# Low parts of every second weight tile by an adding DMA from SBUF to SBUF instead of by VectorE

## The chip, the cores and the metric

The kernel runs on one core of one Trainium2 chip. The metric is the device time of one execution in microseconds; the kernel before has a median of 1213.01 us over three runs. One further execution was profiled, and its trace is what is read below.

## What is computed

Four layers of a transformer trunk on 256 tokens of width 1024, all in float32. Each layer has a token mixer (banded attention in layers 0 and 3, gated linear attention in layer 1, differential attention in layer 2), a layer norm, a SwiGLU feed-forward network of hidden width 2816, and another norm. Cut to what matters:

```python
for i in range(DEPTH):                      # 4
    y = mixer(h)                            # x @ w_qkv (or w_in), attention, @ w_o
    h = layer_norm(DN_ALPHA * h + y, ln1_g[i], ln1_b[i])
    g, u = split(h @ ffn_w_gate_up[i])      # [1024, 2 * 2816]
    h = layer_norm(DN_ALPHA * h + (silu(g) * u) @ ffn_w_down[i], ln2_g[i], ln2_b[i])
```

Most of the time is products of 256 tokens with weights that are each read once, 392 tiles of 256 x 512 elements (512 KB).

## The kernel before

**Split products.** TensorE multiplies in float32r, a rounded form of float32. To keep the accuracy, every operand is split into a high part (the value rounded to float32r) and a low part (what the rounding lost). A product is the sum of three: high by low, high by high, low by high. `w_tiles` (L101) makes the parts of a weight tile, which is two k-tiles of 128 rows by 512 columns, so 128 partitions x 1024 elements in SBUF. Its steps: a DMA from SP's queue into `raw` (L109), ScalarE's copy, which rounds it into `wh` (L110), and VectorE's subtraction of the two into `wl` (L111). There are RAWB = 6 buffers for `raw` and WB = 8 each for `wh` and `wl`. The first two tiles (`fine`) are handled one k-tile at a time.

**Row form** (`run_rows`, L141). Tokens stand on the partitions of the result, 512 columns fill a bank. For each token half and k-tile three products are issued: L175 with the low part, L176 and L177 with the high part. Half 1 runs LAG = 10 k-tiles behind half 0, so that each weight tile stays in its buffer for some six tiles' time. This form serves the value projections, the first two chunks of the gate-and-up weights, the output projections (`out_proj`, in an order of its own), and the down projection `w_down`, whose two chunks of 22 k-tiles are 22 tiles per layer, 88 in all. Gated linear attention uses it too, partly with a lag of 4.

**Column form** (`run_cols`, L182). 128 columns of the weights stand on the partitions of the result and all 256 tokens are in the free dimension. The four tiles of a 512-column chunk are made first; then each of four blocks runs over all 8 k-tiles (L196 with the high part, L197 with the low). So a buffer comes free in the last block of its chunk, and eight buffers hold two chunks. Nine chunks of each feed-forward network (36 in all), four of each attention and one of the gated layer run in this form.

**Order of the work.** Work that follows from a finished product is put off by counted half-steps (`defer`, `tick`). The order on each engine is fixed when the kernel is built, by a list scheduler that goes by priorities in program order and by a model of times. On the chip each engine then works through its queue in order and waits on semaphores. A buffer that is taken over makes its writer wait until the last reader of the old contents is done.

**GpSimd's queue** carries little: the layer norms' `rstd_of` (L245, L249, each on a few columns), masks (L408), and the loads of `late_load` (L122 and L123: norm weights, attention biases), which are its only DMAs. Its DMAs are the software queue q0 in the profile; the weight loads from SP are q1.

Of the kernel before, what the change touches and what calls it, by code (L numbers as in the profile page):

```python
# [12 lines left out]
ALU = mybir.AluOpType  # L13
# [12 lines left out]
RAWB = 6  # weight loads under way, 2 k-tiles each  # L26
WB = 8  # split weights on chip, 2 k-tiles each
LAG = 10  # k-tiles that token half 1 runs behind half 0
# Half-steps of the tensor engine (see run_rows) by which work is put off.
# [6 lines left out]
def trunk_kernel(  # L36
# [27 lines left out]
    nc = tc.nc  # L64
# [35 lines left out]
    # ---------------------------------------------------------------- weights  # L100
    def w_tiles(chunk, s, fine=False):  # L101
        """Loads the k-tiles 2s, 2s+1 of a 512-column chunk of the weights and
        returns, per k-tile, their float32r parts (high, low)."""
        raw = wp.tile([P, 2, 512], F32, tag="raw", bufs=RAWB, name=nm("raw"))
        wh = wp.tile([P, 2, 512], F32R, tag="wh", bufs=WB, name=nm("wh"))
        wl = wp.tile([P, 2, 512], F32R, tag="wl", bufs=WB, name=nm("wl"))
        src = chunk[s].rearrange("p (k n) -> p k n", k=2)
        for k in (slice(0, 1), slice(1, 2)) if fine else (slice(0, 2),):
            nc.sync.dma_start(raw[:, k, :], src[:, k, :])  # L109
            nc.scalar.copy(out=wh[:, k, :], in_=raw[:, k, :])  # L110
            nc.vector.tensor_tensor(  # L111
                out=wl[:, k, :],
                in0=raw[:, k, :],
                in1=wh[:, k, :].bitcast(F32),
                op=ALU.subtract,
            )
        return [(wh[:, k, :], wl[:, k, :]) for k in range(2)]

    def late_load(dst, src, seen):
        """A load that is needed late, held back until `seen` is written, to  # L120
        leave the DMA queues to the weights."""
        nc.gpsimd.tensor_copy(dst[:, 0:1], seen)  # L122
        nc.gpsimd.dma_start(dst, src)  # L123

    # Work of the mixers that follows from a finished product is put off by a
    # number of half-steps (one k-tile of 512 columns for one token half), so
    # that the tensor engine has products to run while its inputs are made.
# [13 lines left out]
    def run_rows(chunks, lag=LAG, order=None, fine=0):  # L141
        """Products in row form (tokens on partitions, 512 columns a bank).
        chunks: (weights, k-tiles, src, done); src(kt) gives the high | low
        k-tile of all tokens, done(t, bank) reads the finished product.
        order lists (token half, chunk, k-tile); without it token half 1 runs
        lag k-tiles behind half 0."""
# [35 lines left out]
    def run_cols(w, src, done):  # L182
        """Products in column form: 128 columns of the weights on partitions,
        all 256 tokens in the free dimension. The bank of a column block holds
        the product with the tokens' high parts | with their low parts (high
        weights only), to be added up."""
        wt = []
        for s in range(NKT // 2):
            wt += w_tiles(w, s)
        for blk in (0, 2, 1, 3):  # L190
            b = bank("mm")
            cs = slice(blk * P, (blk + 1) * P)
            for kt in range(NKT):
                wh, wl = wt[kt]
                xk = src(kt)
                nc.tensor.matmul(b, wh[:, cs], xk, start=kt == 0, stop=False)  # L196
                nc.tensor.matmul(  # L197
                    b[:, :256], wl[:, cs], xk[:, :256], start=False, stop=kt == NKT - 1
                )
                if kt == NKT - 1:  # L200
                    done(blk, b)
                if kt % 2:
                    tick(1)
# [3 lines left out]
    # ------------------------------------------------------------- transposes  # L207
    def put(dst, ks, cs, val):
        """Writes val as the high and low parts of k-tiles ks, tokens cs."""
        h = dst[:, ks, cs]  # L210
        nc.scalar.copy(out=h, in_=val)  # L211
        nc.vector.tensor_tensor(  # L212
            out=dst[:, ks, slice(256 + cs.start, 256 + cs.stop)],
            in0=val,
            in1=h.bitcast(F32),
            op=ALU.subtract,
        )

    def split_T(src_cols, dst, t, k0, n):
        """Transposes n [128,128] blocks (row form in src_cols) into the k-tiles  # L220
        k0.. of token half t of dst."""
# [12 lines left out]
    def operand():  # L234
        """High | low parts of 8 k-tiles of all tokens."""
        return slab([P, NKT, 4 * P], F32R)
# [4 lines left out]
    # ------------------------------------------------------------- layer norm  # L241
# [12 lines left out]
    class Norm:  # L254
# [12 lines left out]
        def load(self, seen):  # L267
            """The next of the loads that the norm waits for."""
            if self.loads:
                late_load(*self.loads.pop(0), seen)  # L270
# [61 lines left out]
    def out_proj(OT, w, norm):  # L332
        """The k-tiles that need the last of the mixer's output come late, and
        enough of half 1 after half 0 to cover the norm of half 0."""
# [10 lines left out]
    # ------------------------------------------------- banded softmax attention  # L345
    def attention(xT, wqkv, bias_ap, w_o, norm, diff, src=None, **first):
        """One column block of 128 holds two 64-wide score maps: two heads, or
        the two maps of one differential head."""
# [133 lines left out]
        def turn2(c, pr):  # L482
            """Key block 0: half 0 of both heads, half 1 of both; key block 1:
            half 1 of both heads."""
# [17 lines left out]
        def values2(c, ph, pl):  # L502
            """Values of both heads against the weights of each: the rows of
            the other head are not read."""
# [101 lines left out]
    # ------------------------------------------------- gated linear attention  # L606
    def gla(xT, norm):
# [21 lines left out]
        # Low-rank gate: the columns 0..15 of the stationary tile are the high  # L629
        # parts of w_g1 and 32..47 the low parts (what follows them, the next  # L630
        # k-tile's, gives rows that nothing reads); w_g2 stands in the same
        # rows, so that the second product adds both up, and its bias in row 64.
# [209 lines left out]
    # ----------------------------------------------------------------- swiglu  # L842
# [52 lines left out]
    # ------------------------------------------------------------------ trunk  # L895
# [36 lines left out]
def _layouts(inputs):  # L932
    """Weights laid out chunk by chunk as the kernel reads them, x also with
    its tokens last, and the relative-position tables laid out per (query
    partition p, key column c): the key sits c - 128 - p places after the query."""
# [4 lines left out]
    def tiles(w, pairs=0):  # L940
        """[L, K, N] to [L, chunk, K / 256, 128, 2 * 512]; the first `pairs`
        chunks hold 256 columns of each of the first two parts of that width."""
# [68 lines left out]
```

## Time and profile before

| | |
|---|---|
| median of 3 runs (lowest to highest) | 1213.01 us (1209.94 to 1214.02) |
| span of the profiled execution, first to last instruction | 1209.5 us |
| TensorE busy | 1191.5 us, 99% |
| VectorE busy | 829.6 us, 69% |
| ScalarE busy | 665.5 us, 55% |
| GpSimd busy | 97.7 us, 8% |
| DMA queue q1 (weights), share of 16 engines | 52.1% for 207.64 MB |
| DMA queue q0 (GpSimd's), share | 3.5% for 15.14 MB |
| mean granted TensorE clock, share of full | 0.998 |

Where the profile gives a time of one instruction, it is in ns in the groups and in us in the timelines. A busy TensorE is not TensorE at its peak, as products are pipelined and their ends are modelled; the pace is read from the starts. An idle time in brackets belongs to the engine just before the instruction, with what ended it. The profile gives no time of the profiled execution but its span; the runs' median is 3.5 us above it.

### The profile page before, as it was taken

To read this page: it belongs to the slowest core of one execution; us is meant where nothing else is said; L and a number is where in the kernel's file an instruction comes from. 1 tells how busy PE (TensorE), PEld (TensorE's weight loads), DVE (VectorE), ACT (ScalarE), POOL (GpSimd) and SP (SyncE) were. 2 spreads that over 40 slices of the span, in tenths; PEclk is the share of its full clock that TensorE was granted. 3 is DMA by queue.
4 is the path that set the end of the run, shared out by engine and by line. 5 is a ranking of instruction groups with operands and counts; after the bars stand their busy time and mean duration, and the time that the engine had idled before them with its cause. 6 is when DMAs were issued, how large, how long until landed. Compare 5 with 4: busy or idle time off the path is not lost.

```text
span 1209.5 us, 17080 instructions
## 1 busy us (share of the span) xinstructions
PE 1191.5 (99%) x6224; PEld 993.6 (82%) x6224; DVE 829.6 (69%) x1418; ACT 665.5 (55%) x1169; POOL 97.7 (8%) x188
## 2 busy tenths in 40 slices
PE   7999999999999999999999999999999999999997
PEld 5888888888887888888887778888888888888885
DVE  6687866745656777764667787676466888666644
ACT  6566555643664455663446656556344774665531
POOL 0130000000101000000012110000001200000000
PEclk9999999999999999999999999999999999999999
DMA  9654646556464456555564355665557544655641
GB/s 340 225 189 140 210 173 226 175 176 194 155 229 136 137 195 230 193 184 187 189 226 152 122 168 188 225 198 171 188 185 235 188 126 156 205 208 197 205 143 35
DMA packets 62772, 223.88 MB, mean 185 GB/s; under 512 B 7264, under 2 KB 7776, under 8 KB 62688
## 3 DMA queue, kind: packets, MB, share of 16 engines
q1 hardware_dynamic: 58176, 207.64, 52.1%
q0 software_dynamic: 4512, 15.14, 3.5%
q8 instruction: 49, 0.80, 0.3%
q14 instruction: 35, 0.29, 0.1%
HBM read 221.71 MB, written 1.05 MB: 184 GB/s over the span
## 4 chain that ended last, share of the span: by engine, by line
PE 94%; DVE 2%; ACT 2%; DMA 1%; POOL 0%; issue 0%; SPq 0%; POOLq 0%; DVEq 0%; ACTq 0%
PE mm L196 28%; PE mm L175 15%; PE mm L176 15%; PE mm L197 15%; PE mm L177 15%; PE tp L422 2%; PE tp L224 2%; ACT k L445 1%; PE tp L491 1%; DVE k L430 1%; DMA raw<-in_a_qkv_dram 1%; DVE wl L111 0%; PE tp L512 0%; PE tp L514 0%; PE tp L513 0%
## 5 line engine op out<-in xcount | busy, mean ns | idle before, releaser
L111 DVE TENSOR_TENSOR wl<-raw,wh 128x1024 fp32r<-128x1024 f32 (+1 forms) x394 | 476.0, 1214 | 180.6 <-ACT wh L110 177.7
L196 PE MATMUL mm<-slab,wh 128*128 128x512 f32 x1568 | 555.6, 397 | 0.0
L110 ACT CAST wh<-raw 128x1024 fp32r<-128x1024 f32 (+1 forms) x394 | 406.4, 1047 | 196.7 <-PE mm L177 185.2
L197 PE MATMUL mm<-slab,wl 128*128 128x256 f32 x1568 | 440.8, 281 | 0.0
L196 PEld LDWEIGHTS mm<-slab,wh 128*128 128x128 f32 x1568 | 294.3, 188 | 71.1 <-issue 4.6
L175 PE MATMUL mm<-wl,slab 128*128 128x512 f32 x784 | 311.5, 397 | 7.9 <-DVE wl L111 7.9
L177 PE MATMUL mm<-wh,slab 128*128 128x512 f32 x784 | 307.4, 392 | 0.0
L176 PE MATMUL mm<-wh,slab 128*128 128x512 f32 x784 | 307.2, 392 | 0.0
L197 PEld LDWEIGHTS mm<-slab,wl 128*128 128x128 f32 x1568 | 296.5, 189 | 0.7 <-issue 0.3
L175 PEld LDWEIGHTS mm<-wl,slab 128*128 128x128 f32 x784 | 147.8, 189 | 41.1 <-DVE wl L111 8.5
L177 PEld LDWEIGHTS mm<-wh,slab 128*128 128x128 f32 x784 | 147.6, 188 | 31.7 <-DVE slab L212 0.8
L176 PEld LDWEIGHTS mm<-wh,slab 128*128 128x128 f32 x784 | 147.8, 189 | 30.4 <-issue 1.8
L869 DVE TENSOR_TENSOR k<-mm,k 128x256 f32<-128x256 f32 x144 | 60.6, 421 | 82.9 <-ACT k L868 82.9
L868 ACT COPY k<-mm 128x256 f32<-128x256 f32 x144 | 53.7, 373 | 71.4 <-PE mm L197 71.1
L871 ACT ACTIVATE k<-k 128x256 f32<-128x256 f32 x72 | 29.8, 414 | 46.7 <-DVE k L869 46.7
L245 POOL TENSOR_SCALAR sm<-mv 128x1 f32<-128x1 f32 x16 | 14.1, 883 | 500.4 <-DVE mv L300 500.4
L211 ACT CAST slab<-k 128x256 fp32r<-128x256 f32 (+1 forms) x76 | 31.8, 418 | 40.9 <-DVE k L875 37.4
L212 DVE TENSOR_TENSOR slab<-k,slab 128x256 fp32r<-128x256 f32 (+1 forms) x76 | 33.0, 435 | 23.1 <-ACT slab L211 23.1
L445 ACT ACTIVATE k<-k,nmx 128x128 f32<-128x128 f32 x96 | 42.5, 444 | 8.4 <-DVE nmx L441 8.3
L211 ACT CAST slab<-tp 128x512 fp32r<-128x512 f32 (+1 forms) x56 | 27.1, 495 | 26.6 <-PE tp L224 24.5
L430 DVE CUSTOM_DVE_ANT_0 k<-tp,k 128x128 f32<-128x128 f32 x96 | 28.6, 353 | 10.1 <-PE tp L422 9.0
L212 DVE TENSOR_TENSOR slab<-tp,slab 128x512 fp32r<-128x512 f32 (+1 forms) x56 | 30.6, 569 | 4.6 <-ACT slab L211 4.5
(133 smaller groups left out, 669.5 us busy)
## 6 DMA issues: line engine op xcount, KB each, us to landing
raw<-in_w_gu_dram SPq DMA_DIRECT2D x176, 512.0 KB, 4.4
raw<-in_w_down_dram SPq DMA_DIRECT2D x88, 512.0 KB, 4.2
raw<-in_a_qkv_dram SPq DMA_DIRECT2D x46, 512.0 KB, 4.7
raw<-in_b_in_dram SPq DMA_DIRECT2D x24, 512.0 KB, 3.6
raw<-in_c_qkv_dram SPq DMA_DIRECT2D x24, 512.0 KB, 3.6
raw<-in_a_o_dram SPq DMA_DIRECT2D x16, 512.0 KB, 3.9
k<-in_a_bias_dram POOLq DMA_DIRECT2D x16, 256.0 KB, 4.5
lng<-in_ln_g_dram POOLq DMA_DIRECT2D x8, 512.0 KB, 5.7
```

The source lines that it names most:

```text
L110: nc.scalar.copy(out=wh[:, k, :], in_=raw[:, k, :])
L111: nc.vector.tensor_tensor(out=wl[:, k, :], in0=raw[:, k, :], in1=wh[:, k, :].bitcast(F32), op=ALU.subtract,)
L175: nc.tensor.matmul(b, xh, wl, start=first, stop=False)
L176: nc.tensor.matmul(b, xh, wh, start=False, stop=False)
L177: nc.tensor.matmul(b, xl, wh, start=False, stop=last)
L196: nc.tensor.matmul(b, wh[:, cs], xk, start=kt == 0, stop=False)
L197: nc.tensor.matmul(b[:, :256], wl[:, cs], xk[:, :256], start=False, stop=kt == NKT - 1)
L211: nc.scalar.copy(out=h, in_=val)
L212: nc.vector.tensor_tensor(out=dst[:, ks, slice(256 + cs.start, 256 + cs.stop)], in0=val, in1=h.bitcast(F32), op=ALU.subtract,)
L445: nc.scalar.activation(pr[:, m, SL[t]], pr[:, m, SL[t]], AF.Exp, bias=nmx[:, t, m : m + 1], accum_out=sm[:, t, m : m + 1],)
L868: nc.scalar.copy(out=lo, in_=b[:, 256:])
L869: nc.vector.tensor_tensor(out=lo, in0=b[:, :256], in1=lo, op=ALU.add)
```

## The change

`w_tiles` numbers its tiles. For tiles with an even number above 8 that are not `fine`, VectorE's subtraction is left out. ScalarE writes the negated raw tile, rounded to float32r, into `wl` (which is the negated high part), and a DMA issued on GpSimd's queue adds `raw` onto it, from SBUF to SBUF, so that `wl` holds raw minus high again. The other tiles are as before. Comments and docstrings were also blanked out, and the added lines move all lines behind them by a few; that part of the diff is left out here.

```diff
+    units = [0]
+
     def w_tiles(chunk, s, fine=False):
...
         src = chunk[s].rearrange("p (k n) -> p k n", k=2)
+        units[0] += 1
+        by_dma = not fine and units[0] > 8 and units[0] % 2 == 0
         for k in (slice(0, 1), slice(1, 2)) if fine else (slice(0, 2),):
             nc.sync.dma_start(raw[:, k, :], src[:, k, :])
             nc.scalar.copy(out=wh[:, k, :], in_=raw[:, k, :])
+            if by_dma:
+                nc.scalar.mul(wl[:, k, :], raw[:, k, :], -1.0)
+                nc.gpsimd.dma_start(wl[:, k, :], raw[:, k, :], accum_op=ALU.add)
+                continue
             nc.vector.tensor_tensor(
                 out=wl[:, k, :],
                 in0=raw[:, k, :],
```

## Rows read from the trace of the kernel before

**Rows 1.** The page's first part: busy us, share of the span, instructions.

```profile
PE 1191.5 (99%) x6224; PEld 993.6 (82%) x6224; DVE 829.6 (69%) x1418; ACT 665.5 (55%) x1169; POOL 97.7 (8%) x188
```

**Rows 2.** TensorE's waits: engine line <- releaser: us in total, times, longest us.

```profile
PE mm L175 <- DVE wl L111: 7.9, 2, 6.5
...
PEld tp L578 <- DVE k L565: 2.8, 7, 0.9
...
PEld tp L422 <- DVE slab L396: 2.6, 10, 0.4
...
PEld tp L224 <- DVE h L319: 1.1, 4, 0.3
```

**Rows 3.** The page's costliest groups: busy us, mean ns | idle before, releaser.

```profile
L111 DVE TENSOR_TENSOR wl<-raw,wh 128x1024 fp32r<-128x1024 f32 (+1 forms) x394 | 476.0, 1214 | 180.6 <-ACT wh L110 177.7
...
L110 ACT CAST wh<-raw 128x1024 fp32r<-128x1024 f32 (+1 forms) x394 | 406.4, 1047 | 196.7 <-PE mm L177 185.2
```

**Rows 4.** Timeline of ScalarE in layer 1's down projection: start us, us, what, idle before.

```profile
562.51 1.05 ACT L110 CAST wh<-raw 128x1024 fp32r<-128x1024 f32 x1 [1.67 <-PE mm L177]
565.23 1.05 ACT L110 CAST wh<-raw 128x1024 fp32r<-128x1024 f32 x1 [1.67 <-PE mm L177]
```

**Rows 5.** Timeline of all engines there: two steps of half 0 and half 1.

```profile
567.71 0.39 PE L175 MATMUL mm<-wl,slab 128*128 128x512 f32 x1
...
568.39 0.39 PE L175 MATMUL mm<-wl,slab 128*128 128x512 f32 x1
```

**Rows 6.** Timeline of ScalarE over one chunk of layer 1's gate-and-up columns.

```profile
484.36 1.05 ACT L110 CAST wh<-raw 128x1024 fp32r<-128x1024 f32 x1
...
486.88 2.00 ACT L110 CAST wh<-raw 128x1024 fp32r<-128x1024 f32 x2
...
497.71 0.37 ACT L868 COPY k<-mm 128x256 f32<-128x256 f32 x1
```

**Rows 7.** Stretches: columns, down projection, attention, flat-out loads; columns as headed.

```profile
core 0: us, PE busy (x) PEld busy (x) DVE busy (x) ACT busy (x) POOL busy (x), PEclk, DMA share, GB/s
456.00:522.00 66.00, 66.00 (x383) 58.17 (x382) 45.96 (x73) 41.06 (x72) 2.48 (x4) 1.00 0.61 205
552.00:592.00 40.00, 40.00 (x179) 33.11 (x178) 20.95 (x19) 15.44 (x15) 0.00 (x0) 1.00 0.58 183
40.00:106.00 66.00, 65.93 (x399) 53.96 (x398) 54.68 (x170) 45.87 (x123) 13.85 (x35) 1.00 0.56 184
...
15.00:40.00 25.00, 25.00 (x122) 20.84 (x122) 18.88 (x19) 15.13 (x18) 3.11 (x10) 1.00 0.90 346
```

**Rows 8.** DMA: queue's packets, MB, share; issues, KB, us to landing; the last of 552:592.

```profile
q1 hardware_dynamic: 58176, 207.64, 52.1%
...
lng<-in_ln_g_dram POOLq DMA_DIRECT2D x8, 512.0 KB, 5.7
...
h<-in_x_dram POOLq DMA_DIRECT2D x2, 512.0 KB, 4.2
k<-in_c_bias_dram POOLq DMA_DIRECT2D x8, 128.0 KB, 3.6
...
raw<-in_w_down_dram SPq DMA_DIRECT2D x8, 512.0 KB, 3.5
```

**Rows 9.** GpSimd: its costliest groups, its waits, and a norm's start in its timeline.

```profile
L123 POOL DMA_DIRECT2D k<-in_a_bias_dram x16 | 8.9, 555 | 2.0 <-POOL k L122 2.0
...
POOL k L408 <- DMA k<-in_a_bias_dram: 54.4, 16, 5.9
...
596.37 1.11 POOL L245 TENSOR_SCALAR sm<-mv 128x1 f32<-128x1 f32 x1 [57.42 <-DVE mv L300]
```

## The prediction, made before the changed kernel was run

> **What bounds the kernel now.** I read first how busy each engine is [rows 1]: TensorE is busy for 1191.5 of a span of 1209.5 us, so only 18 us of it are idle, and those include the start and the end. VectorE has 829.6 us of work and ScalarE 665.5 us, neither near the span. The second view is what TensorE and its weight loads wait for [rows 2]: the products of L175 wait for the low parts `wl` twice, 7.9 us in all, of which 6.5 us is one wait at the very start (tile 2 of the first stage, which the change leaves with VectorE, since only tiles after the eighth are touched). The other waits on VectorE are 2.8, 2.6 and 1.1 us in total. So VectorE's subtractions (394 of them, 476.0 us [rows 3]) are hidden almost entirely: taking half of them away frees an engine that nobody waits for. What can still matter is whether the new way to a low part is longer than the cover that the old way has. So the third view is the timeline of the stage with the least cover.
>
> That stage is the down projection. `run_rows` runs token half 1 ten k-tiles (five weight tiles) behind half 0, and there are eight split buffers. So tile i takes over the buffer of tile i-8, which half 1 leaves two tiles before half 0 needs tile i. In the timeline, ScalarE's copy of one tile starts at 562.51 right after it waited 1.67 us for a product of L177 to free the buffer, and the next at 565.23, so one tile lasts 2.72 us [rows 4]. The tile copied at 562.51 is first used by the L175 product at 567.71; the k-tiles that lie between are four of half 0 and four of half 1, 24 products, at 0.68 us for three [rows 5], which is 5.44 us counted from the end of the freeing product. From the start of the copy to the use there are 567.71 - 562.51 = 5.2 us. Before, 1.05 us of copy and 1.22 us of subtraction [rows 3] fill 2.3 us of that, and 2.9 us are spare. This cover, 5.2 us, is the number that decides.
>
> In the column stages the cover is longer. One chunk is four tiles and its buffers come free during the last block of the chunk before. The copy of a chunk's first tile starts at 484.36, its last pair of copies at 486.88 (so the fourth at 487.8), and the chunk is first used at about 497.4, just ahead of L868's copy of the previous chunk's last block at 497.71 [rows 6]. That is 13.0 us for the first tile. The fourth tile is used six k-tiles into its first block, about 2.1 us later (a block of eight is a quarter of a chunk, 2.76 us), so it has 11.7 us.
>
> **The change, part by part.**
>
> *VectorE.* Of 392 tiles those with an even number above 8 go to the new way: 192. VectorE loses 192 x 1.224 = 235 us, worth nothing by itself by [rows 2], at most the 6.5 us of the three waits above that are not at the start.
>
> *ScalarE.* It gains 192 multiplications of 128x1024. Its copy of the same shape takes 1.05 us [rows 3]; I take the same, 202 us, 867 in all. The work that hides them: the column stage at 456 to 522 us has 41.1 us of ScalarE in 66, which becomes 41.1 + 12 x 1.05 = 53.7; the attention stage 45.9 in 66, and eight multiplications make it 54.3 [rows 7]. Both stay below 83%, so I cost it at nothing. Were that cover gone it would be up to 1.05 us per tile on the path.
>
> *The path of a new low part.* Copy 1.05, multiplication 1.05, about 0.1 for two signals, then the adding DMA from issue on GpSimd's queue to landing. No row shows an adding DMA. The nearest: a plain 512 KB load from GpSimd's queue lands in 4.2 us (`h`), one of 128 KB in 3.6 us and a broadcast of 512 KB in 5.7 us; weight loads in the down projection land in 3.5 us [rows 8]. An addition must read its target as well as its source, so I add one more pass of 512 KB through the 16 DMA engines. A pass costs, by q1's row [rows 8], 52.1% of 1209.5 us for 207.64 MB, or 1.59 us for 512 KB, and in the stretch where the loads run flat out, share 0.90 at 346 GB/s [rows 7], 346/0.90 = 384 GB/s, or 1.37 us. So from below 4.2 (the second read hidden), from above 5.7 + 1.6 = 7.3, and below 3.5 would be without any precedent here. I take 4.2 + 1.37 = 5.6 us, nearest to the row of `h`, the same size on the same queue. The path is then 2.2 + 5.6 = 7.8 us, with ends of 6.4 and 9.5.
>
> The Trainium skill (DMA: Bandwidth & Descriptors, Anatomy of one DMA) gives a fit for GpSimd's DMAs of 2.0 us plus the bytes at 436 GB/s, which is 3.2 us for 512 KB. Row and rule differ: the plain one of that size took 4.2 us here. By the rule the path would be 5.4 us and the down projection would lose next to nothing; that is the second rival below.
>
> *Down projection.* The path of 7.8 us against a cover of 5.2 us leaves 2.6 us. A stall of one new tile also lengthens the cover of the next new one, two tiles on, because the buffer that this one needs is freed just ahead of the place of the first stall. So stalls come at every second new tile, not at each. Of 22 tiles per layer the last 14 have the short cover, seven of them new: four stalls of 2.6 us, four layers: 16 x 2.6 = 42 us (ends: 16 x 1.2 = 19 and 16 x 4.3 = 69). Loads of raw tiles have room: a raw buffer is now held until the DMA has landed, some 2.6 us past the old time, but it is refilled six tiles (16 us) ahead and a load takes 3.5 us.
>
> *DMA engines.* A chunk of a column stage has four loads and two additions: 4 x 1.37 + 2 x 2.74 = 11.0 us of all 16 engines, in the 11.05 us that the chunk takes, if a read of the target costs a full pass. With the loads at 1.59 it is 12.7; with an addition at one pass it is 8.2. If the engines can be kept 95% busy (between the 0.90 of the flat-out stretch and full), 11.0 becomes 11.5, so 0.5 us per chunk. The feed-forward layers have 36 such chunks: 18 us (ends 0 and 36 x 1.7 = 61). Attention's chunks last half as long again and are left out; in the down projection the stalls already leave the engines this time.
>
> *GpSimd's queue.* Each addition is one more issue, 0.55 us by L123's row [rows 9], and waits in order for its multiplication. Behind it stand the layer norm's two steps (L245, L249) and the late loads. The norm's chain has no spare: its L245 started at 596.37, at once [rows 9], and TensorE's transposes already wait 0.3 us for L319 four times [rows 2]. A norm that meets a waiting issue is late by up to 2 x 1.05 us; there are 16, the bounds are 0 and 34 us, and I take a quarter, 8 us, since only some will meet one. In attention an issue can also stand behind L408's wait of up to 5.9 us for a bias [rows 9]; the cover there is over 13 us as in the column stage, so nothing.
>
> *Sum:* 42 + 18 + 8 = 68 us on a span of 1209.5, or 1277.5. The median of the three runs is 1213.0, 3.5 us above that span, so 1281 us.
>
> **The rivals.**
>
> *The DMA engines become the bound.* If an addition costs three passes (both reads and the write), a chunk needs 4 x 1.37 + 2 x 4.1 = 13.7 us, at 95% 14.4 instead of 11.05. That is 3.4 us times 36, or 122 us; two tiles of the row stages need 6.8/0.95 = 7.2 instead of 5.44, 1.75 us for each of some 44 pairs of the down projections, 77 us; 200 in all, about 1413 us. For it: the share is already 0.58 to 0.61 in these stages and 3.18 us of two passes per 5.5 us is alone 0.58 more [rows 7]. Against it: I see no row in which the writing side of a load costs time of its own. The Trainium skill (Collectives: The Full Stack, Why ReduceScatter is half of AllGather) says that an addition in a DMA is slower because it needs two source reads and not because of the arithmetic. By that rule it is two passes and the sum above stands; no row here can show it.
>
> *Not slower: the landing fits the cover.* The place is the down projection, and the point is an issue-to-landing time of 3.0 us: below it the path is 5.2 us and no tile is late. Then only VectorE's relief is left, the waits of 6.5 us less what the norms lose, so 1207 to 1213 us. For it: no loads but its own run in that stage, and source and target are both on chip. Against it: not even the 128 KB transfer of that queue landed in under 3.6 us, and the target has to be read first.
>
> *The change does not do what it says.* If the scheduler delays the GpSimd issues or VectorE still carries the work, VectorE's row of L111 would still count 394 and the time would be that of before, 1213 us.
>
> **How the numbers follow.** Forecast, stalls of the down projection with small additions (1235 to 1325): 0.58. DMA engines the bound (1325 to 1450): 0.30. Landing fits: 0.10, of which 0.04 end faster and 0.06 within 0.3%. Not as said: 0.02, no change. A measurement of this kernel can tell about 0.3% from no change. So faster 0.04, same 0.08, slower 0.88. The range from 1225 to 1420 leaves out the 0.12 of no change and below and some 0.07 at the top; it takes in the low end of the landing time (19 us alone, 1232) and the price of the first rival.
>
> **What would show it.** In the profile of the changed kernel, L111 with 202 instructions, 192 of ScalarE's multiplications at 1.05 us and 192 more issues on GpSimd, with 5.6 us to landing. In the down projection, TensorE waiting in L175 for a DMA into `wl`, 2 to 3 us, at every second new tile, with the granted clock at its upper level. In the column stages a DMA share near 0.95 and few waits. The forecast is wrong if the landing takes 3 us or less, or 8 us and more; if TensorE's waits lie in L196 and L197; or if the transposes of L224 carry most of the loss.

## The result, and the profile after

The changed kernel takes 1354.67 us (median of three runs, 1348.56 to 1360.02) against 1213.01: the ratio is 1.117 with a 95% interval from 1.112 to 1.122, or 142 us more. The prediction was 1281 us, in a range from 1225 to 1420. So the direction was right and the size was not: 142 us were lost where 68 were forecast.

The profiled run lasted 1360.0 us with a span of 1358.3. First the page of the changed kernel: busy time (us, share, instructions), the DMA queues (packets, MB, share of the 16 engines), the costliest groups (busy us, mean ns | idle before, releaser) and the issues of the new DMA (KB, us to landing). The low-part products of L175 and L197 are L183 and L205 here, the copy of L110 is L114, the subtraction of L111 is L119; L116 is the new multiplication and L117 the adding DMA.

```profile
PE 1239.8 (91%) x6224; PEld 1015.9 (75%) x6224; DVE 624.1 (46%) x1226; ACT 832.5 (61%) x1361; POOL 250.1 (18%) x380
...
q1 hardware_dynamic: 58176, 207.64, 44.2%
q0 software_dynamic: 32160, 115.82, 43.5%
...
L119 DVE TENSOR_TENSOR wl<-raw,wh 128x1024 fp32r<-128x1024 f32 (+1 forms) x202 | 244.5, 1212 | 312.7 <-ACT wh L114 312.4
...
L117 POOL DMA_DIRECT2D wl<-raw x192 | 166.2, 867 | 872.5 <-ACT wl L116 692.1
...
L116 ACT ACTIVATE wl<-raw 128x1024 fp32r<-128x1024 f32 x192 | 203.8, 1062 | 52.3 <-PE mm L183 47.5
...
wl<-raw POOLq DMA_DIRECT2D x192, 512.0 KB, 7.2
```

The change did what it says: 192 low parts moved, VectorE went from 829.6 to 624.1 us [rows 1], ScalarE gained 192 x 1.062 us. TensorE has the same 6224 products as before, but the span is 148.8 us longer: 100.5 us of that is more idle time (118.5 against 18.0), and 48.3 us is the same products taking longer (1239.8 against 1191.5). These are two losses, and the forecast had only the first.

The next view is what TensorE waits for in the changed kernel (us in total, times, longest us), beside the few waits of before [rows 2].

```profile
PE mm L183 <- DMA wl<-raw: 55.1, 28, 5.1
PE mm L205 <- DMA wl<-raw: 39.2, 23, 4.1
PE mm L183 <- DVE wl L119: 7.3, 2, 6.9
...
PE tp L232 <- DVE h L327: 0.6, 2, 0.3
```

94.3 us of the idle time are 51 waits for the adding DMA, in two places: the row products (L183) and the column products (L205). The wait of 6.9 us at the start is the old one. The norm's transposes (L232) wait 0.6 us, less than before.

By stage, from the first product of a stage's first tile to that of the next, the feed-forward columns of the four layers went from 102.0, 100.1, 102.0, 100.1 to 117.9, 112.2, 115.0, 114.0 us (+55), the down projections from 60.9, 60.9, 60.9, 68.5 to 78.1, 83.8, 75.1, 81.9 (+68), and the rest gained some 26. For layer 1, the columns and then the down projection, first in the kernel before and then in the changed one (headed as in [rows 7]: length, busy time of TensorE, its loads, VectorE, ScalarE and GpSimd, granted clock, DMA share, GB/s):

```profile
441.70:541.80 100.10, 100.10 (x579) 88.22 (x578) 68.20 (x106) 60.52 (x107) 3.56 (x6) 1.00 0.60 204
541.80:602.70 60.90, 60.90 (x274) 50.30 (x273) 35.87 (x44) 27.68 (x30) 2.06 (x2) 1.00 0.58 183
```

```profile
489.70:601.90 112.20, 105.00 (x580) 90.56 (x579) 50.86 (x89) 74.87 (x125) 18.78 (x23) 0.97 0.96 262
601.90:685.60 83.70, 69.56 (x274) 54.95 (x273) 23.95 (x33) 37.55 (x42) 11.10 (x14) 0.90 0.81 213
```

In the kernel before, TensorE was busy for the whole of both stretches, at a clock of 1.00. Now the down projection has 83.70 - 69.56 = 14.1 us of idle time, and its products take 69.56 - 60.90 = 8.7 us longer, at a clock of 0.90 (a tenth of 83.7 is 8.4 us). The DMA share is 0.81 there and 0.96 in the columns.

TensorE's waits for the addition in the four down projections, layer by layer:

```profile
PE mm L183 <- DMA wl<-raw: 10.9, 6, 3.2
...
PE mm L183 <- DMA wl<-raw: 14.1, 6, 5.1
...
PE mm L183 <- DMA wl<-raw: 10.9, 6, 3.1
...
PE mm L183 <- DMA wl<-raw: 7.5, 4, 3.4
```

So the +68 us of the down projections are 43.4 us of waits and 24 us of slower products (TensorE is busy for 266.8 us in these four stretches, 242.7 before). In the feed-forward columns the waits in L205 are 10.7, 7.2, 9.5 and 8.7 us, 36.1 in all, and the slower products are 19 us (423.0 against 404.1).

**The down projection, wait by wait.** TensorE's timeline in layer 0's down projection, from 280 to 327 us (start, us, instruction, idle before): all waits for the addition, and two products between them.

```profile
280.20 0.50 PE L183 MATMUL mm<-wl,slab 128*128 128x512 f32 x1 [3.20 <-DMA wl<-raw]
...
281.95 0.63 PE L183 MATMUL mm<-wl,slab 128*128 128x512 f32 x1
...
285.35 0.39 PE L183 MATMUL mm<-wl,slab 128*128 128x512 f32 x1
...
293.44 0.50 PE L183 MATMUL mm<-wl,slab 128*128 128x512 f32 x1 [0.43 <-DMA wl<-raw]
...
302.44 0.76 PE L183 MATMUL mm<-wl,slab 128*128 128x512 f32 x1 [3.24 <-DMA wl<-raw]
...
315.58 0.50 PE L183 MATMUL mm<-wl,slab 128*128 128x512 f32 x1 [0.66 <-DMA wl<-raw]
...
324.47 0.50 PE L183 MATMUL mm<-wl,slab 128*128 128x512 f32 x1 [3.14 <-DMA wl<-raw]
```

A new tile is due every eight products of L183, 5.44 us. The waits are at two of three: 3.2 us, none, 0.5 us, and again. GpSimd's issues of the additions behind them, from the same timeline:

```profile
288.51 0.85 POOL L117 DMA_DIRECT2D wl<-raw  x1 [12.60 <-ACT wl L116]
293.94 0.85 POOL L117 DMA_DIRECT2D wl<-raw  x1 [4.59 <-ACT wl L116]
300.13 0.85 POOL L117 DMA_DIRECT2D wl<-raw  x1 [5.34 <-ACT wl L116]
```

They land 4.9, 8.4 and 4.8 us after the issue, and the next three likewise (5.1, 8.6, 4.8). The issue at 288.51 lands just ahead of the product of 293.44, the one at 293.94 ahead of that of 302.44. The landing of 8.4 us is the wait of 3.24 us.

The longer landing is the one that meets weight loads. SP's queue of loads stands still while an addition holds the raw buffer that the next load needs (between 285 and 330 us it waits six times for a landing, 30.7 us in all). The addition issued at 288.51 landed at 293.4, and SP at once issued two loads, at 293.45 and 293.87, just ahead of the addition of 293.94:

```profile
293.45 0.80 SPq L113 DMA_DIRECT2D raw<-in_w_down_dram  x2
```

The DMA queues (packets, MB, share of the 16 engines) from 294.5 to 298.0 us, and from 298.5 to 301.0:

```profile
q1 hardware_dynamic: 215, 0.81, 88.3%
...
q0 software_dynamic: 118, 0.47, 94.4%
q1 hardware_dynamic: 34, 0.08, 8.5%
```

In the first stretch GpSimd's queue q0 has no packet (it isn't in the view): the addition moves only when the two loads are nearly through. While the additions that landed in 4.8 to 5.1 us were under way, the engines served loads for 0.4 to 1.5 us, at most the time of one. Over all 192 additions the time to landing goes with the engine time of the loads served meanwhile (a correlation of 0.84, from the packets of the trace). Why the loads go first is not shown.

**The path.** ScalarE in the same stage, for the new tile of 293.44:

```profile
287.15 1.06 ACT L116 ACTIVATE wl<-raw 128x1024 fp32r<-128x1024 f32 x1 [1.31 <-PE mm L183]
288.12 1.03 ACT L114 CAST wh<-raw 128x1024 fp32r<-128x1024 f32 x1
```

The multiplication stands before the copy of the same tile. It waits for the last reader of the old low part (L183); the last reader of the old high part, for which the copy has to wait, is L185 of the same step, two products later. So the copy isn't on the path. From the start of the multiplication the addition is issued 1.36 us later and lands after another 4.9 us, against a cover of 293.44 - 0.43 - 287.15 = 5.9 us: 0.4 us late. With a landing of 8.4 us, and a cover that the short wait has lengthened to 6.6 us, it is the wait of 3.24 us.

**The clock.** The product at 281.95, after the wait of 3.20 us, takes 0.63 us and the one at 285.35 takes 0.39. Two stretches of the same length there, headed as above:

```profile
281.40:284.80 3.40, 3.40 (x9) 2.63 (x9) 0.00 (x0) 0.01 (x1) 0.00 (x0) 0.50 0.99 252
285.00:288.40 3.40, 3.40 (x17) 2.77 (x16) 1.23 (x1) 2.09 (x3) 0.00 (x0) 1.00 0.39 139
```

In both TensorE is busy throughout, with 9 products at a granted clock of 0.50 (1.2 GHz) and 17 at 1.00 (2.4 GHz). The clock is at the lower level after each of the waits of 3.20, 3.24 and 3.14 us in this stage, and not after those of 0.43 and 0.66. The wait of 3.20 us so brings a second loss of about half its size, the 3.40 us at half speed that follow it. Over the whole run the mean granted clock is 0.97 against 0.998, so (1 - 0.97) x 1358.3 - 0.002 x 1209.5 = some 38 us, which is most of the 48.3 us by which the products grew.

Not every long wait is followed by the lower level. Of the 13 waits for an addition that are longer than 3 us, ten end in such a stretch or less than 2 us ahead of one, and three don't. One of the three is the wait of 3.35 us in layer 1's columns; the stretch right behind it:

```profile
518.50:521.90 3.40, 3.40 (x19) 2.98 (x20) 0.42 (x1) 1.67 (x3) 0.85 (x1) 1.00 1.04 289
```

**The columns.** One chunk of layer 1's columns in the changed kernel: the two multiplications of ScalarE, the copy of the chunk's fourth tile, the two issues, and the product of the fourth tile.

```profile
528.08 1.07 ACT L116 ACTIVATE wl<-raw 128x1024 fp32r<-128x1024 f32 x1
...
529.44 0.85 POOL L117 DMA_DIRECT2D wl<-raw  x1 [7.59 <-ACT wl L116]
...
530.28 1.05 ACT L114 CAST wh<-raw 128x1024 fp32r<-128x1024 f32 x1
...
531.49 1.07 ACT L116 ACTIVATE wl<-raw 128x1024 fp32r<-128x1024 f32 x1
...
532.85 0.85 POOL L117 DMA_DIRECT2D wl<-raw  x1 [0.63 <-ACT k L879]
...
545.01 0.58 PE L205 MATMUL mm<-slab,wl 128*128 128x256 f32 x1 [3.42 <-DMA wl<-raw]
```

The product was ready to run at 545.01 - 3.42 = 541.6, so from the start of the copy the cover is 11.3 us, about what the prediction counted (11.7). The second addition lands 12.1 us after its issue, and that alone is more. The queues' shares in these 12.1 us (532.85 to 544.96):

```profile
q0 software_dynamic: 418, 1.52, 62.4%
q1 hardware_dynamic: 528, 1.90, 39.8%
```

So the engines were full throughout, with 4.8 us of weight loads and 7.6 us of GpSimd's queue, of which an addition's own are 2.9 (experiment 2); the rest are the end of the first addition, a late load and the start of the next addition. Of the additions issued in this stage the first of two lands in 6.2 to 8.3 us and the second in 6.6 to 12.1.

### The profile page after: what moved, and what is told of

It is laid out like the page before. It is cut to its first block, busy times and chain, and to the rows that moved or that the text cites. A ratio compares the mean times of both kernels' runs of the same rounds, so it can differ in the third digit from the quotient of the medians.

```text
span 1358.3 us, 17440 instructions
## 1 busy us (share of the span) xinstructions
PE 1239.8 (91%) x6224; PEld 1015.9 (75%) x6224; DVE 624.1 (46%) x1226; ACT 832.5 (61%) x1361; POOL 250.1 (18%) x380
## 3 DMA queue, kind: packets, MB, share of 16 engines
q0 software_dynamic: 32160, 115.82, 43.5%
HBM read 221.71 MB, written 1.05 MB: 164 GB/s over the span
## 4 chain that ended last, share of the span: by engine, by line
PE 44%; DMA 24%; issue 19%; ACT 7%; POOL 3%; DVE 2%; SPq 0%; POOLq 0%; DVEq 0%; ACTq 0%
DMA wl<-raw 20%; PE mm L204 14%; PE mm L205 7%; PE mm L183 6%; PE mm L185 6%; PE mm L184 6%; ACT wh L114 3%; ACT wl L116 2%; DMA k<-in_c_bias_dram 1%; POOL wl L117 1%; PE tp L430 1%; DMA raw<-in_b_in_dram 1%; PE tp L232 1%; PE tp L499 1%; ACT k L453 1%
## 5 line engine op out<-in xcount | busy, mean ns | idle before, releaser
L204 PE MATMUL mm<-slab,wh 128*128 128x512 f32 x1568 | 570.1, 405 | 0.0
L114 ACT CAST wh<-raw 128x1024 fp32r<-128x1024 f32 (+1 forms) x394 | 406.1, 1041 | 188.3 <-PE mm L185 108.4
L205 PE MATMUL mm<-slab,wl 128*128 128x256 f32 x1568 | 449.8, 287 | 39.3 <-DMA wl<-raw 39.2
L119 DVE TENSOR_TENSOR wl<-raw,wh 128x1024 fp32r<-128x1024 f32 (+1 forms) x202 | 244.5, 1212 | 312.7 <-ACT wh L114 312.4
L183 PE MATMUL mm<-wl,slab 128*128 128x512 f32 x784 | 323.9, 413 | 62.7 <-DMA wl<-raw 55.1
L204 PEld LDWEIGHTS mm<-slab,wh 128*128 128x128 f32 x1568 | 301.0, 192 | 73.3 <-issue 4.6
L205 PEld LDWEIGHTS mm<-slab,wl 128*128 128x128 f32 x1568 | 302.9, 193 | 48.5 <-DMA wl<-raw 47.7
L117 POOL DMA_DIRECT2D wl<-raw x192 | 166.2, 867 | 872.5 <-ACT wl L116 692.1
L184 PE MATMUL mm<-wh,slab 128*128 128x512 f32 x784 | 314.4, 401 | 0.0
L185 PE MATMUL mm<-wh,slab 128*128 128x512 f32 x784 | 314.2, 401 | 0.0
L116 ACT ACTIVATE wl<-raw 128x1024 fp32r<-128x1024 f32 x192 | 203.8, 1062 | 52.3 <-PE mm L183 47.5
L183 PEld LDWEIGHTS mm<-wl,slab 128*128 128x128 f32 x784 | 152.5, 195 | 108.3 <-DMA wl<-raw 59.3
L185 PEld LDWEIGHTS mm<-wh,slab 128*128 128x128 f32 x784 | 151.8, 194 | 33.7 <-issue 0.2
L184 PEld LDWEIGHTS mm<-wh,slab 128*128 128x128 f32 x784 | 152.9, 195 | 30.2 <-issue 1.1
L284 DVE SCALAR_TENSOR_TENSOR h<-h,mm 128x512 f32<-128x512 f32 x32 | 21.9, 683 | 41.1 <-PE mm L185 41.1
```

What stands on the lines that cost most here:

```text
L116: nc.scalar.mul(wl[:, k, :], raw[:, k, :], -1.0)
L117: nc.gpsimd.dma_start(wl[:, k, :], raw[:, k, :], accum_op=ALU.add)
L119: nc.vector.tensor_tensor(out=wl[:, k, :], in0=raw[:, k, :], in1=wh[:, k, :].bitcast(F32), op=ALU.subtract,)
L183: nc.tensor.matmul(b, xh, wl, start=first, stop=False)
L184: nc.tensor.matmul(b, xh, wh, start=False, stop=False)
L185: nc.tensor.matmul(b, xl, wh, start=False, stop=last)
```

## The experiments

The theory was: the loss is the landing of the additions, later than the cover of their tile in the down projection and in the columns, and TensorE's lower clock behind the longer waits. The rivals: full DMA engines, which hold up the loads and everything else whether or not a product waits for an addition; and ScalarE, which has 204 us more to do. Ratios and differences are to the median of the kernel before on the same occasion (1212.11 us for experiments 1 to 3, 1210.87 for 4, 6 and the first run of 7, 1211.70 for 5, 8 and the second run of 7).

**1. The multiplications alone**, without the DMA behind them.

```diff
                 nc.scalar.mul(wl[:, k, :], raw[:, k, :], -1.0)
-                nc.gpsimd.dma_start(wl[:, k, :], raw[:, k, :], accum_op=ALU.add)
                 continue
```

> Leaves the adding DMA out: every second low part is only the negated high part. Theory (a landing that is later than the cover, plus DMA engines nearly full in the column stages, plus a lowered TensorE clock after each stall): ScalarE's 204 us of multiplications are hidden, so 1205 to 1218 us, clock 0.99 or more, no wait of L183 or L205 on a low part beyond the 7 us at the start. Rival A (ScalarE's added work or its place in the queue is the cost): 1280 us or more. Rival B (the 16 DMA engines are the bound everywhere): as the theory.

1212.68 us, 1.001 times the kernel before (1.000 to 1.002). Without the DMA, ScalarE's 192 multiplications more and VectorE's 192 subtractions less (623.6 us busy against 829.6) together come out at nothing. So the additions have nothing to win here: at best they cost nothing.

**2. A copying DMA in place of the adding one.** Source, target, queue and wait are the same.

```diff
-                nc.gpsimd.dma_start(wl[:, k, :], raw[:, k, :], accum_op=ALU.add)
+                nc.gpsimd.dma_start(wl[:, k, :], raw[:, k, :])
```

> The DMA copies raw onto the low part and doesn't add, so that it reads one source and not two; issue, queue, size and multiplications stay. Theory: the pass costs 1.3 to 1.6 us of the 16 engines instead of 2.8, a column chunk needs 8.2 to 9.3 us of 11.05, so the column stages lose nothing; in the down projection the landing falls to about 5 us and some stalls stay: 1220 to 1250 us, DMA share about 0.72. Rival B: with the share down, 1213 to 1220. Rival C (the fixed delay of GpSimd's queue is the cost, not the engines' time): 1310 us or more. Rival A: 1340 or more.

1247.56 us, 1.029 (1.026 to 1.032). The waits of TensorE, and after them the time to landing, shortest, median and longest:

```profile
PE mm L183 <- DMA wl<-raw: 21.1, 19, 3.8
...
PE mm L205 <- DMA wl<-raw: 4.9, 5, 2.4
```

```profile
DMA to landing us min/median/max: 2.9/5.6/10.0
```

For the changed kernel the last line reads:

```profile
DMA to landing us min/median/max: 4.5/7.2/12.4
```

The columns are nearly back, at 100.2 to 105.1 us (100.1 to 102.0 before), and the down projections at 66.5 to 72.6. So 107 of the 142 us come with the adding, and 35 with a move of 512 KB by that queue at all. The price in engine time: the queue's share of 43.5% of 1358.3 us, less the 42 us that it had before (3.5% of 1209.5), over 192 is 2.86 us of all 16 engines for an addition; for the copy, 26.6% of 1245.0 less 42 over 192 is 1.5 us. The Trainium skill (Collectives: The Full Stack, Why ReduceScatter is half of AllGather) says of a collective's addition in a DMA that it is slower because of its second source read. These two numbers agree with it, at 1.9 times.

**3. A longer cover in the down projection**, in the changed kernel and, as a control, in the kernel before: half 1 runs six k-tiles behind half 0 and not ten, so that buffers come free two tiles earlier.

```diff
-            ]
+            ],
+            lag=6,
         )
```

> The changed kernel with token half 1 six k-tiles behind half 0 in the down projection and not ten, so that a buffer comes free two weight tiles earlier and the cover there grows from 5.2 to about 10.6 us. Theory: the four down projections fall from 75 to 84 us each to 62 to 68, so 1290 to 1305 us, while the column stages keep their loss. Rival B: the engines' time is the same, so 1340 us or more.

> The kernel before with the same lag of six in the down projection, as the control: the norm of half 0 loses some of its cover, 0 to 3 us per layer, so 1212 to 1225 us by every theory.

The changed kernel with it takes 1301.53 us (1.074, 1.071 to 1.076), the kernel before 1218.57 (1.006, 1.004 to 1.008). The same edit takes 53 us off the one and adds 6 to the other. Waits and layer 1's down projection of the changed kernel with it:

```profile
PE mm L205 <- DMA wl<-raw: 42.9, 27, 3.9
PE mm L183 <- DMA wl<-raw: 12.4, 7, 2.6
```

```profile
589.30:653.50 64.20, 61.22 (x274) 50.22 (x273) 23.32 (x33) 38.30 (x42) 11.33 (x15) 1.00 0.99 285
```

The waits in L183 fell from 55.1 to 12.4 us, those in L205 stayed. The stage is 64.2 us long and not 83.7, at a clock of 1.00 and with a DMA share of 0.99. The bytes and additions are the same, and the engines were fuller than before. So the down projection's loss was cover (the four are 9 us longer than before, 7 longer than in the control), and engines that are full to 0.99 cost little there.

**4. The additions only in the columns, and only in the rows.**

```diff
-        by_dma = not fine and units[0] > 8 and units[0] % 2 == 0
+        by_dma = not fine and units[0] > 8 and units[0] % 2 == 0 and cols
```

(`cols` is set by `run_cols`; the other run has `and not cols`.)

> Only the tiles of the column form go the new way, those of the row form stay with VectorE. Theory: the column stages keep their loss (guC stages 112 to 118 us instead of 100 to 102) and the down projections are back at 61 us each: 1265 to 1290 us. If the two losses feed each other through the DMA queues: under 1255.

> Only the tiles of the row form go the new way. Theory: the down projections keep their loss of 54 to 70 us in all, the feed-forward columns are back at 100 to 102 us each: 1270 to 1290 us. The loss of this kernel and of the one with columns alone add up to that of both, 142 us, within 15.

Columns alone: 1276.38 us, 1.054 (1.051 to 1.056), +65. Rows alone: 1303.34 us, 1.075 (1.072 to 1.079), +92, more than was expected. The sum, 158, is 16 above the 142 of both, just outside the 15 that were expected, so the two losses stand side by side, with a small overlap. In the run with rows alone the down projections account for +65, as in the changed kernel. The other 30 us are in stages that the expectation had left out: the values of layers 2 and 3 (+11), the gated layer's rows (+6) and the first tiles of gate and up (+12 over the four layers), about half of it with waits of 2.5 to 3.2 us in L183 at the first row tiles after a change of stage. Another part is no wait for an addition. At the start of layer 2 TensorE's transposes wait 3.6 us for a norm, whose step L257 stands in GpSimd's queue behind the issue of an addition that itself waits for ScalarE:

```profile
658.39 0.88 POOL L117 DMA_DIRECT2D wl<-raw  x1 [3.20 <-ACT wl L116]
659.00 0.86 POOL L257 TENSOR_TENSOR sm<-sm,powt 128x1 f32<-128x1 f32 x1
```

**5. The additions in the columns, at the other places of the chunk.** As in the run with columns alone, with two additions per chunk, but tiles 1 and 3 (of 0 to 3, the second and the fourth) are made first, ahead of tiles 0 and 2. Each product uses the tiles in the old order.

```diff
+        made = {s: w_tiles(w, s, cols=s % 2 == 1) for s in (1, 3, 0, 2)}
         for s in range(NKT // 2):
-            wt += w_tiles(w, s)
+            wt += made[s]
```

> Only column tiles go the new way, as in the run with columns alone (1276 us), and the same two of each chunk, but these two are loaded, multiplied and added first and the other two after them, so that the addition which came last starts some 2 us earlier. Same loads, same additions, same bytes. If the loss of the columns is a landing later than its cover: most stalls of 1 to 4 us there shrink by 1 to 2 us, 1225 to 1255 us. If the engines' time sets the pace: 1270 to 1282, no change.

1230.74 us, 1.017 (1.014 to 1.020), against 1276.38. Layer 1's columns, first with the additions in the old places, then in the new:

```profile
459.80:574.90 115.10, 105.87 (x580) 90.59 (x579) 53.07 (x91) 73.64 (x123) 17.55 (x22) 0.97 0.94 259
```

```profile
453.00:555.00 102.00, 102.00 (x580) 88.46 (x579) 53.05 (x92) 73.77 (x123) 15.33 (x21) 1.00 1.00 291
```

TensorE's 9.2 us of idle time are gone and the clock is 1.00, although the landings did not get shorter (median 8.3 us against 7.4) and the DMA share rose to 1.00. So in the columns, too, the loss was cover. What is left over the four layers is 9 us, with single stages of 100.1 or 102.0 us in the kernel before.

**6. Full engines without anybody waiting.** VectorE makes all low parts as in the kernel before, and the same 192 additions run as bystanders, each from a raw tile onto itself after both of its readers; no product reads the outcome. Their place on GpSimd's queue is the same.

```diff
+        if by_dma:
+            nc.gpsimd.dma_start(raw, raw, accum_op=ALU.add)
```

> All low parts by VectorE as in the kernel before; for the same 192 tiles an adding DMA of the same size adds the raw tile onto itself after both its readers are done, and nobody waits for it except the next load into that buffer. It loads the 16 engines as the change does, without the longer path. If the engines' time sets the pace of the column stages: 0.5 to 1.5 us per chunk, so 1230 to 1270, with ScalarE waiting for raw loads, and next to nothing in the down projections. If the path past the cover is all there is to it: 1211 to 1220.

1243.35 us, 1.026 (1.021 to 1.030). Layer 1's columns and one wait of ScalarE:

```profile
449.60:554.10 104.50, 102.18 (x579) 88.41 (x578) 68.68 (x107) 60.14 (x109) 18.43 (x23) 1.00 1.03 291
```

```profile
ACT wh L114 <- DMA raw<-in_w_gu_dram: 68.5, 41, 4.2
```

Full engines do delay the loads, for which ScalarE now waits, and cost 32 us, beside the 142 of the change, in this form (a bystander also holds its raw buffer until it has landed). In the columns they cost 104.6 + 104.5 + 100.1 + 103.6 - 404.2 = 9 us, as much as was left in the run before. (A share is the sum of the packets' times, and can come out above 1.) The forecast of this run was split: 1230 or more if engine time is the loss, up to 1220 if it is the path alone. It came out between the two theories: mostly the path, and engine time for about a fifth, if the change pays for its full engines what the bystander pays; no run separates that.

**7. Half as many additions**, every fourth tile, and then with the lag of six as well.

```diff
-        by_dma = not fine and units[0] > 8 and units[0] % 2 == 0
+        by_dma = not fine and units[0] > 8 and units[0] % 4 == 0
```

> Every fourth tile and not every second goes the new way, 96 additions. Theory (a threshold, not a price per addition): a column chunk needs 4 x 1.54 + 2.65 = 8.8 us of the engines in 11.05, so no loss there; in the down projection a landing of about 5 us makes the path some 0.7 to 1 us longer than the cover for three or four tiles per layer: 1220 to 1232 us in all. A price per addition (142/192 = 0.74 us each) gives 1284.

> Every fourth tile by DMA and the lag of six in the down projection. By the theory no column stage and no down projection has a landing past its cover; what stays is the stalls of about 3 us at the first row tiles after an attention or output projection: 1222 to 1235 us. If half the additions cost half whatever their cover: 1270 to 1285.

1246.84 us (1.028, 1.025 to 1.031), above the 1220 to 1232 expected, and 1236.70 (1.021, 1.018 to 1.024) with the shorter lag. Half of the additions cost a quarter of the loss, 36 us of 142: the columns, now with one addition per chunk, are at 100.1 to 104.1 us. The one that is kept is that of the fourth tile, which waited before; with no other addition in its chunk, TensorE's waits in L205 are 4.6 us and not 39.2. But the down projections still take 64.7 to 72.7, with 18 waits in L183 (21.8 us in all). The shorter lag takes these to 3 (6.4 us), and the time ends just above the 1222 to 1235 expected.

**8. Both remedies with all 192 additions**: the places of experiment 5 for every column chunk and the lag of six.

> Both remedies in the changed kernel with its 192 additions: lag of six in the down projection, and the two new tiles of a column chunk first. By cover alone the gain adds up: 1302 us less what the other run gains on 1276, so 1250 to 1280 us; never below the control with that lag, 1218.6, since VectorE's relief was worth nothing with the DMA left out (1212.7 against 1212.1).

1258.71 us, 1.037 (1.034 to 1.041). TensorE's largest wait for an addition is what remains in the row products, at the first tiles after a change of stage among others:

```profile
PE mm L183 <- DMA wl<-raw: 17.2, 12, 3.1
```

So 96 us of the loss go with two changes of cover that leave the number of bytes and of additions as it was. The 47 us that remain are of the size of the bystander's 32 plus these waits; the 6 us of the control with that lag may be among them, and no run takes them apart. None of the versions is faster than the kernel before, and experiment 1 leaves them nothing to gain.

## Why the prediction was right and wrong

*That VectorE's relief is worth nothing and ScalarE's work is hidden*: right, shown by experiment 1 for the two together.

*That the cover of the low parts decides, with the down projection first*: right, shown by experiment 3: +68 us there in the changed kernel, and +9 with two more tiles of cover.

*The waits of the down projection, 16 x 2.6 = 42 us*: measured are 43.4 us, but the working was not right, so the closeness is in part luck. The path held the copy (1.05 us), which ScalarE makes after the multiplication there. The landing was taken as 5.6 us, nearest to a lone load of the same size; in layer 0 it is 4.8 to 5.1 us or 8.4 to 8.6, as loads stand before it or not. And the waits aren't 2.6 us at every second new tile: in layers 0 and 1 they come at two of three, one long and one short, and there are 22 in all.

*The clock, with no term*: this is one step that failed. The prediction wanted the waits "with the granted clock at its upper level" and priced a wait at its length. The rows show it at 0.50 at the end of ten of the 13 waits of more than 3 us, or shortly behind. The products took 48.3 us longer, of which the mean clock accounts for some 38. 24 us of the 48.3 lie in the down projections and 19 in the columns. No run separates the clock from the waits; where the waits went (experiments 3 and 5), it went back to 1.00.

*The columns, 18 us*: this is the other step that failed. The forecast gave the columns a price by engine time alone (11.0 us of engines in 11.05 us of chunk), with few waits, since a path of 7.8 us fits into 11.7. The engine time was right: 2.86 us for an addition against the 2.74 assumed, a share of 0.96 against 0.95. But the same landing of 5.6 us, taken from loads that ran alone, was put into a stage whose engines the same paragraph filled to 95%. The two additions of a chunk stand 3.4 us apart among four loads, and the second landed in up to 12.1 us in layer 1. In the chunk shown the cover was then too short by 3.4 us. Over the four layers TensorE waited 36.1 us, and the stages grew by 55. The prediction named its own test, waits in the column products' low parts; 39.2 us of them stand in L205. Experiment 5 shows that it was the cover and not the engines: same additions, 9 us.

*The first rival (1413 us)*: an addition doesn't take three passes but 1.9 (experiment 2), and engines that are full cost 32 us (experiment 6), not 200. That the time came out in this rival's band (1325 to 1450) is no support for it.

*The second rival (landing within the cover)*: the Trainium skill's fit (DMA: Bandwidth & Descriptors, Anatomy of one DMA), 3.2 us for 512 KB, is near the shortest landing of the copy, 2.9 us. It differs from the copy's median beside the loads (5.6 us) and from all landings of the addition (4.5 us at the least).

*Norms behind GpSimd's queue, 8 us*: the delay is there and TensorE doesn't pay for it. VectorE's step of the norm (L327) waits 8.7 us for GpSimd, in 13 places (0.4 us before), but the norm's transposes wait 0.6 us in all. With additions in the rows alone one such wait does reach TensorE, 3.6 us (experiment 4).

*What else had no term*: the first row tiles after a change of stage, and attention's and the gated layer's columns, which together are most of some 26 us outside the two stages.

Together, the span grew by 148.8 us where 68 were forecast: 43.4 us of waits for the additions in the down projections (42 forecast), 36.1 in the feed-forward columns (18, for the engines' time), 14.8 of them elsewhere (none), 6.2 of other idle time (8, for the norms) and 48.3 of slower products (none).

## What to carry to other kernels

When work moves from an engine to a DMA, compare the cover of each tile with the landing that the DMA will have in that stage, among its loads and beside the other DMA of the same chunk, and not with the landing of a lone transfer; a sum of engine time that just fits did not say that the landings would be hidden: here they spread from 6.6 to 12.1 us for the second addition of a chunk. Ask too which loads the landing itself sets free, since here they went ahead of the next addition. Look for the stage with the least cover, but check the others again with the longer landing. And price a wait of TensorE of a few microseconds above its length: here the products after most of the waits of over 3 us ran for a while at half the clock.

## What the runs showed of the hardware

An adding DMA of 512 KB within SBUF took 2.86 us of all 16 DMA engines, the copy of the same size 1.5. It landed in 4.5, 7.2 and 12.4 us (shortest, median, longest), the copy in 2.9, 5.6 and 10.0. GpSimd is busy for 0.87 us with the issue of an addition and for 0.54 with that of a copy. With a DMA share of 1.00 in layer 1's columns (experiment 5) TensorE had no idle time, 102.00 us busy in 102.00, as long as the columns of layers 0 and 2 took without any addition (102.0). After a wait of 3.20 us TensorE ran nine products in the time of seventeen (a granted clock of 0.50 against 1.00), after the waits of 0.43 and 0.66 us in the same stage it did not, and neither did it after one of 3.35 us in another. An addition issued just behind two weight loads had no packet on the engines from 294.5 to 298.0 us, until they were nearly through, and landed in 8.4 us (the two were issued 0.5 and 0.1 us before it); one with 0.5 us of loads beside it landed in 4.8.
